# Differential values computed tile by tile in 512-column products, and the last output row tile gathered in SBUF and scaled in two pieces

## The chip, the cores and the metric

One core of one Trainium2 chip runs the whole program. The metric is the device time of one execution in microseconds; the figure given for a kernel is the median of its runs.

## The reference, cut to what matters

Two layers of a hybrid encoder act on a sequence of 512 rows and 1024 columns; a final RMSNorm follows. All values are float32.

```python
for i in range(DEPTH):                                   # 2 layers
    h = rmsnorm(x, norm_mix[i])
    proj = h @ w_in[i]
    qa, ka, va, glu_in, qc, kc, vc, gates = jnp.split(proj, SPLITS, axis=-1)
    ya = diff_attention(qa, ka, va, ...)                 # 4 heads; va is 512 x 512
    yb = conformer_conv(glu_in, ...)
    yc = neighbourhood_attention(qc, kc, vc, rpb[i])     # 8 heads
    ga, gb, gc = jnp.split(jax.nn.sigmoid(gates), 3, axis=-1)
    merged = ga * (ya @ w_br_a[i]) + gb * (yb @ w_br_b[i]) + gc * (yc @ w_br_c[i])
    x = x + merged @ w_o[i]
    h = rmsnorm(x, norm_ffn[i])
    x = x + (silu(h @ w_ffn_gate[i]) * (h @ w_ffn_up[i])) @ w_ffn_down[i]
    h = rmsnorm(x, norm_ple[i])
    x = x + sigmoid(h @ w_ple_gate[i]) * (p[i] @ w_ple_in[i])
return rmsnorm(x, norm_final)
```

The change touches two places of it: `va`, the values of the differential attention, and the very last line, the output rows `x * factor * gain`, where the factor of a row is `(mean(x*x) + EPS) ** -0.5`.

## The kernel before

**Precision.** Every matrix product is made from three: a float32 operand is split into a high half (a rounded copy, made by ACT) and a low half (the difference, made by DVE), and hi x hi, hi x lo and lo x hi are added up in PSUM. `split` is that pair of operations, one on ACT and one on DVE. `weights` loads a block of 128 x 1024 weights by SyncE and splits it; it uses three SBUF pools of three buffers each, `wr` (raw), `wh` and `wl` (the halves), and marks its instructions as 400 steps more urgent than the place where they are written. A buffer is free for the next block when its last reader is done.

**Who sets the order.** TensorE works in the order in which the code is written. The code itself interleaves two kinds of units with the large products: `later` queues an attention unit, and each fourth `chunk` of a product is a `tick` that starts a due unit or takes a running one a step further. A unit of the neighbourhood attention ("natten") is: scores, a softmax on DVE and ACT, transposes, the copies `natten_pt` of the transposed probabilities to SBUF (a high half by ACT, a low half by DVE), the products `natten_av`, and at the end `natten_y`. A unit of the differential attention is built alike. On ACT, DVE and POOL a scheduler orders the instructions by their dependencies and urgency, and each of these engines then works strictly in that order.

**PSUM.** There are eight banks: three named `mm`, two `sc` (scores), two `tr` (transposes), one `av`.

**The values.** `values` (L605) is called by `diff_v` (L830) twice in a layer (L455, L459), each time for two heads, that is 256 columns: four calls in all. A call takes two `mm` banks as accumulators (called `diff_mm`), each for two of the four tiles of 128 rows. The weights come in two loads of four chunks, 1024 columns each. For every chunk and tile there are three products of 256 columns: h's high half with the weights' high half (L621), the same with the weights' low half (L623), h's low half with the weights' high half (L625); 96 in all. When the last is done, four copies on ACT and four subtractions on DVE split the sums into `diff_v`. Around the first call of a layer lie the query and key products of a head (`diff_in`; their rotary embedding makes `diff_rp`, `diff_t` and `diff_kh` on DVE, with `diff_rp` first filled by a DMA), natten units, and behind it the next head's products and a gate (`gatec`).

**The end.** `final` (L1283) makes the last gated embedding and the norm row tile by row tile (t = 0 to 3). `finish` makes a row tile's last 256 columns, adds up its squares, and POOL makes the factor of each row (`ple_rc`, a power). `store` scales the other columns out of PSUM (`low`, columns 0 to 511, and the first half of `pair`, columns 512 to 767) and the last 256 (`v`, times factor and gain), and sends the rows to `out`. For t = 3 that is ACT for columns 0 to 511 with a DMA of its own, and two DVE operations of 256 columns with one SyncE DMA each.

## Time and profile before

| what | before |
|---|---|
| median of 3 runs | 1755.69 us (1755.67 to 1756.33) |
| the profiled execution | 1756.09 us, its span 1754.3 us |
| granted TensorE clock | 0.999 |
| matmuls, weight loads | 8970 each, weight loads 1490.2 us (85%) |
| DVE, ACT, POOL | 1421.7 us (81%), 964.4 us (55%), 104.0 us (6%) |
| DMA | 253.82 MB, 145 GB/s on average |

The span runs from the first to the last instruction of the profiled execution; the execution's own time has 1.8 us around it. Busy shares are averages over the whole span, while a stage is bound by whatever it waits for last; so the stages that the change touches are read on their own below.

### The profile page before, as it was taken

The page shows a single profiled execution, that of the slowest core. Times are in us where ns is not written, and L with a number is a line of the kernel's source. Part 1 is how long each engine was busy: PE and PEld are TensorE (multiplying, and loading weights), DVE is VectorE, ACT ScalarE, POOL GpSimd, SP SyncE. Part 2 cuts the span into 40 slices and gives each one's busy share as a digit, 9 for nine tenths or more (in the row PEclk, how much of TensorE's full clock was granted, in tenths as well). Part 3 has the DMA queues.
Part 4 walks back from the last instruction along what each step waited for, and adds up shares of the span by engine and source line. Part 5 has one row for each costly group of instructions (what it writes and reads, how often), then busy time and mean ns, then how long its engine had stood idle before and what let it go on. Part 6 is the DMA issues. An engine that isn't in the chain of part 4 may idle for free.

```text
span 1754.3 us, 25072 instructions
## 1 busy us (share of the span) xinstructions
PE 1747.3 (100%) x8970; PEld 1490.2 (85%) x8970; DVE 1421.7 (81%) x2346; ACT 964.4 (55%) x1729; POOL 104.0 (6%) x114
## 2 busy tenths in 40 slices
PE   9999999999999999999999999999999999999998
PEld 7888888888888888888888898888888988888887
DVE  7967987998799687797776688889887985977876
ACT  5566545226577275574545665553365763745654
POOL 0000000000121020100000000000001210101000
PEclk9999999999999999999999999999999999999999
DMA  6575641334767365543446655323256764755332
GB/s 230 159 192 158 162 126 46 112 100 140 230 162 186 118 171 155 142 119 131 156 130 164 194 150 153 111 73 96 93 176 199 183 172 121 179 143 157 96 105 97
DMA packets 114781, 253.82 MB, mean 145 GB/s; under 512 B 16864, under 2 KB 23776, under 8 KB 114656
## 3 DMA queue, kind: packets, MB, share of 16 engines
q1 hardware_dynamic: 101264, 227.83, 42.3%
q0 software_dynamic: 12672, 23.07, 8.1%
q8 instruction: 71, 1.16, 0.3%
q10 hardware_dynamic: 720, 1.31, 0.2%
q14 instruction: 54, 0.44, 0.1%
HBM read 215.46 MB, written 7.34 MB: 127 GB/s over the span
## 4 chain that ended last, share of the span: by engine, by line
PE 97%; DVE 1%; DMA 1%; ACT 1%; SPq 0%; issue 0%; POOL 0%; POOLq 0%; ACTq 0%; DVEq 0%
PE ffn_mm L1013 6%; PE ffn_sc L1013 6%; PE ffn_mm L180 4%; PE ffn_mm L179 4%; PE ffn_mm L181 4%; PE ffn_mm L1016 3%; PE ffn_sc L1016 3%; PE mergea_mm L180 2%; PE mergea_mm L181 2%; PE mergea_mm L179 2%; PE ffn_tr L1013 2%; PE natten_mm L179 2%; PE natten_mm L180 2%; PE gateb_mm L180 2%; PE gateb_mm L181 2%; PE gateb_mm L179 2%
## 5 line engine op out<-in xcount | busy, mean ns | idle before, releaser
L160 DVE SCALAR_TENSOR_TENSOR conv_z<-glu_z,pre_par,conv_z 128x512 f32<-128x512 f32 x240 | 179.6, 748 | 3.4
L143 ACT ACTIVATE ffn_wh<-ffn_wr 128x1024 fp32r<-128x1024 f32 (+1 forms) x92 | 92.7, 1021 | 99.5 <-PE ffn_mm L180 63.4
L157 DVE TENSOR_TENSOR ffn_wl<-ffn_wr,ffn_wh 128x1024 fp32r<-128x1024 f32 (+1 forms) x92 | 107.1, 1175 | 20.8 <-ACT ffn_wh L143 20.4
L979 POOL DMA_DIRECT2D ffn_qk<-w_fu x88 | 78.0, 992 | 589.3 <-DMA ffn_qk<-w_fu 323.7
L143 ACT ACTIVATE mergea_wh<-mergea_wr 128x1024 fp32r<-128x1024 f32 (+1 forms) x32 | 27.1, 846 | 96.8 <-PE mergea_mm L180 79.6
L157 DVE TENSOR_TENSOR ffn_t<-ffn_mm,wo_rb 128x512 f32<-128x512 f32 (+1 forms) x46 | 31.1, 677 | 51.6 <-PE ffn_mm L181 51.6
L157 DVE TENSOR_TENSOR ffn_wl<-ffn_qk,ffn_wh 128x1024 fp32r<-128x1024 f32 x44 | 53.7, 1220 | 11.0 <-ACT ffn_wh L143 10.9
L143 ACT ACTIVATE diff_a<-diff_sc,diff_s 128x512 f32<-128x512 f32 x32 | 22.0, 688 | 71.6 <-DVE diff_s L893 71.6
L143 ACT ACTIVATE ffn_wh<-ffn_qk 128x1024 fp32r<-128x1024 f32 x44 | 46.7, 1061 | 26.8 <-PE ffn_mm L180 16.2
L179 PE MATMUL ffn_mm<-ffn_v,ffn_wh 128*128 128x512 f32 x132 | 51.4, 389 | 0.0
L180 PE MATMUL ffn_mm<-ffn_v,ffn_wh 128*128 128x512 f32 x132 | 51.4, 389 | 0.0
L181 PE MATMUL ffn_mm<-ffn_v,ffn_wl 128*128 128x512 f32 x132 | 51.3, 389 | 0.0
L179 PE MATMUL ffn_mm<-ffn_y,ffn_wh 128*128 128x512 f32 x132 | 51.3, 389 | 0.0
L180 PE MATMUL ffn_mm<-ffn_y,ffn_wh 128*128 128x512 f32 x132 | 51.3, 389 | 0.0
L181 PE MATMUL ffn_mm<-ffn_y,ffn_wl 128*128 128x512 f32 x132 | 51.3, 389 | 0.0
L143 ACT ACTIVATE natten_wh<-natten_wr 128x1024 fp32r<-128x1024 f32 x24 | 25.4, 1058 | 42.2 <-issue 15.5
L1013 PE MATMUL ffn_sc<-wo_h,ffn_wh 128*128 128x512 f32 x176 | 48.0, 394 | 0.0
L157 DVE TENSOR_TENSOR ffn_t<-ffn_t,ffn_e 128x256 f32<-128x256 f32 x84 | 46.3, 551 | 1.0 <-ACT ffn_e L143 0.9
L893 DVE TENSOR_REDUCE diff_s<-diff_sc 128x1 f32<-128x512 f32 x64 | 42.1, 683 | 2.2 <-PE diff_sc L800 2.2
L1013 PE MATMUL ffn_mm<-wo_h,ffn_wh 128*128 128x512 f32 x160 | 43.6, 394 | 0.0
L225 POOL TENSOR_TENSOR diff_rc<-diff_sm,pre_power 128x4 f32<-128x4 f32 x8 | 8.9, 1115 | 561.8 <-DVE diff_sm L160 503.2
L143 ACT ACTIVATE natten_b<-natten_b,natten_s 128x256 f32<-128x256 f32 x64 | 30.4, 499 | 20.4 <-DVE natten_s L719 20.3
(894 smaller groups left out, 6050.1 us busy)
## 6 DMA issues: line engine op xcount, KB each, us to landing
ffn_qk<-w_fu POOLq DMA_DIRECT2D x88, 256.0 KB, 6.6
ffn_wr<-w_fg SPq DMA_DIRECT2D x44, 512.0 KB, 4.4
ffn_wr<-w_fd SPq DMA_DIRECT2D x32, 448.0 KB, 3.8
ffn_r<-w_fu SPq DMA_DIRECT2D x44, 256.0 KB, 3.1
ffn_qk<-w_fg SPq DMA_DIRECT2D x44, 256.0 KB, 3.3
ffn_qk<-w_fu SPq DMA_DIRECT2D x44, 256.0 KB, 3.4
natten_wr<-w_in SPq DMA_DIRECT2D x16, 512.0 KB, 4.2
diff_wr<-w_in SPq DMA_DIRECT2D x16, 512.0 KB, 4.3
```

The lines of the kernel that those rows point to most:

```text
L143: i = self.nc.scalar.activation(out, in_, func, **kw)
L157: return self.nc.vector.tensor_tensor(out, a, b, op)
L160: return self.nc.vector.scalar_tensor_tensor(out, a, s, b, op0, op1)
L179: mm(out, wh, ah, start=first, stop=False, **kw)
L180: mm(out, wh, al, start=False, stop=False, **kw)
L181: mm(out, wl, ah, start=False, stop=last, **kw)
L225: nc.gpsimd.tensor_tensor(col, ms, self.power, ALU.pow)
L893: nc.vector.tensor_reduce(out=m[:, u:u + 1], in_=sc, op=ALU.max, axis=AX.X, negate=True)
L979: nc.gpsimd.dma_start(q, wu[:, lo], accum_op=ALU.add)
L1013: mm(out, wh[:, c], bs[k][b], start=first and k == 0, stop=False, skip_group_check=True)
L1016: mm(out[:, 0], wl[:, c], bs[k][b][:, 0], start=False, stop=k == 3, skip_group_check=True)
```

## The change

**The values.** A call now issues both weight loads first. Each raw block of four chunks is split into halves that lie side by side, chunk by chunk: 256 columns of the high half, then 256 of the low one. Two chunks fit into a buffer of `wh` and the other two into one of `wl`, so the two loads fill two buffers of each; a call has four splits of 512 columns each in place of two of 1024. The four row tiles are then made one after the other, each in an `mm` bank of its own (before: two banks in all). A tile has eight products of 512 columns, h's high half with both halves of a chunk, and then eight of 256, h's low half with the weights' high half: 64 products in a call where there were 96. The first 256 columns of the bank then hold hi x hi + lo x hi, the second 256 hi x lo. A tile is taken out as soon as it is done: a copy on ACT and a subtraction on DVE as before, and then one more addition on DVE, which adds the second half of the bank to the low half of `diff_v`.

**The end.** For the last row tile the last 256 columns are multiplied by the gain before the factor is there, and the other 768 are copied from PSUM to SBUF by ACT. With the factor, ACT scales columns 0 to 383 and sends them by its own queue, and DVE scales columns 384 to 1023 in one operation, sent by one SyncE DMA. The scaling of columns 512 to 767 of row tile 2 is written ahead of the last `finish`, and row tile 2's low columns go out by SyncE's queue in place of ACT's.

```diff
--- before.py
+++ after.py
@@ -602,37 +602,39 @@
 
         yield from self.norm(st[0], CB, (3, 1), done)
 
-    def values(self, ap, parts):
+    def values(self, ap):
 
 
         mm = self.nc.tensor.matmul
-        accs = [self.ps("mm", (P, 2, 256)) for _ in range(2)]
-        for o in range(0, KD, 4):
-            wh, wl = self.weights(ap[:, o * 256:(o + 4) * 256], 1024)
-            both = [(k, t) for k in range(o, o + 4) for t in range(4)]
-            if o == 0:
-
-                both.sort(key=lambda kt: kt[1] // 2)
-            for n, (k, t) in enumerate(both):
-                s = slice((k - o) * 256, (k - o + 1) * 256)
-                out = accs[t // 2][:, t % 2, :]
-                ts = slice(t * P, (t + 1) * P)
-
-                mm(out, self.h[k][:, 0, ts], wh[:, s], start=k == 0 and t % 2 == 0,
-                   stop=False, skip_group_check=True)
-                mm(out, self.h[k][:, 0, ts], wl[:, s], start=False, stop=False,
+        ws = []
+        with self.tc.high_priority(offset=min(self.w_ahead, self.tc.cur_priority - self.p0)):
+            for o in range(0, KD, 4):
+                raw = self.sb("wr", [P, 2, 2, 256])
+                self.nc.sync.dma_start(raw.rearrange("p a b c -> p (a b c)"),
+                                       ap[:, o * 256:(o + 4) * 256])
+                for n, tag in enumerate(("wh", "wl")):
+                    w = self.sb(tag, [P, 2, 2, 256], F32R)
+                    self.split(w[:, :, 0], w[:, :, 1], raw[:, n])
+                    ws += [w[:, k] for k in range(2)]
+        vs = []
+        for t in range(4):
+            out = self.ps("mm", (P, 2, 256))
+            hs = [(a[:, 0, t * P:(t + 1) * P], a[:, 1, t * P:(t + 1) * P]) for a in self.h]
+            for k, (hi, lo) in enumerate(hs):
+                mm(out, hi, ws[k], start=k == 0, stop=False, skip_group_check=True)
+                if k % 4 == 3:
+                    self.chunk()
+            for k, (hi, lo) in enumerate(hs):
+                mm(out[:, 0], lo, ws[k][:, 0], start=False, stop=k == KD - 1,
                    skip_group_check=True)
-                mm(out, self.h[k][:, 1, ts], wh[:, s], start=False,
-                   stop=k == KD - 1 and t % 2 == 1, skip_group_check=True)
-                if n % 2:
+                if k % 4 == 3:
                     self.chunk()
-        vs = []
-        for acc in accs:
-            v = self.sb("v", [P, 2, 512], F32R)
-            for t in range(2):
-                for hi, lo, a in parts(v[:, t], acc[:, t]):
-                    self.split(hi, lo, a)
-            vs.append(v)
+            if t % 2 == 0:
+                v = self.sb("v", [P, 2, 512], F32R)
+                vs.append(v)
+            hi, lo = v[:, t % 2, 0:256], v[:, t % 2, 256:512]
+            self.split(hi, lo, out[:, 0])
+            self.tt(lo, lo.bitcast(F32), out[:, 1], ALU.add)
         return vs
 
     def natten_in(self, pr, st, ys):
@@ -829,7 +831,7 @@
 
     def diff_v(self, g, st):
         self.phase = "diff"
-        st["v", g] = self.values(self.a["w_va"][self.i, g], lambda v, a: ((v[:, 0:256], v[:, 256:512], a),))
+        st["v", g] = self.values(self.a["w_va"][self.i, g])
 
     def diff_unit(self, head, qt, st4, k2, st, box, ys):
 
@@ -1332,22 +1334,34 @@
             summed.append(self.stt(ms, s, 1.0 / D, part[:, t:t + 1], ALU.mult, ALU.add))
             col = self.sb("rc", [P, 1])
             nc.gpsimd.tensor_tensor(col, ms, self.power[:, 0:1], ALU.pow)
+            if t == 3:
+                self.behind(self.tt(rows[t][:, 768:], v, self.gain, ALU.mult), summed[t])
             vs.append(v)
             columns.append(col)
 
+        def lower(t):
+            nc.vector.tensor_scalar(rows[t][:, 512:768], pair[t][:, 0:256], columns[t], None,
+                                    ALU.mult)
+
         def store(t):
-            col, two = columns[t], pair[t]
+            col = columns[t]
             r, out = rows[t], self.a["out"][t * P:(t + 1) * P]
+            if t == 3:
+                c, d = slice(0, 384), slice(384, D)
+                self.act(r[:, 0:512], low[t], AF.Copy)
+                self.act(r[:, c], r[:, c], AF.Copy, scale=col)
+                nc.scalar.dma_start(out[:, c], r[:, c])
+                nc.vector.tensor_scalar(r[:, d], r[:, d], col, None, ALU.mult)
+                nc.sync.dma_start(out[:, d], r[:, d])
+                return
             self.act(r[:, 0:512], low[t], AF.Copy, scale=col)
-            nc.scalar.dma_start(out[:, 0:512], r[:, 0:512])
+            (nc.sync if t == 2 else nc.scalar).dma_start(out[:, 0:512], r[:, 0:512])
             i = self.stt(r[:, 768:], vs[t], col, self.gain, ALU.mult, ALU.mult)
             if t == 2:
                 self.behind(i, summed[3])
-            if t == 3:
-                nc.sync.dma_start(out[:, 768:], r[:, 768:])
-            nc.vector.tensor_scalar(r[:, 512:768], two[:, 0:256], col, None, ALU.mult)
-            c = slice(512, 768 if t == 3 else D)
-            nc.sync.dma_start(out[:, c], r[:, c])
+            if t < 2:
+                lower(t)
+            nc.sync.dma_start(out[:, 512:], r[:, 512:])
 
         pair, low, pgs, vs, columns, summed = [], [], [], [], [], []
         places = ("av", "mm", "av", "sc")
@@ -1388,6 +1402,9 @@
             pgs.append(pg)
             if t == 1:
                 finish(0)
+            if t == 3:
+                lower(2)
+                self.act(rows[t][:, 512:768], pair[t][:, 0:256], AF.Copy)
             if t:
                 finish(t)
             if t in (1, 2):
```

The order of instructions moves with it. The first place is DVE in the first call of `values` in layer 0. `diff_rp` and `diff_t` are the rotary embedding of the key product just made, `diff_wl_307` is the low half of the weights of the next key product (head 1), `conv_z` belongs to the convolution, and `natten_y` to the natten unit in between. Before:

```order
L160 SCALAR_TENSOR_TENSOR conv_z_81_370<-glu_z_68_321,pre_par_1_67,conv_z_81_370 128x512
L157 TENSOR_TENSOR diff_rp_265_1482<-diff_rp_265_1482,diff_r_235_1323 128x512
L157 TENSOR_TENSOR diff_t_266_1488<-diff_t_266_1488,diff_rp_265_1482 128x512
L157 TENSOR_TENSOR diff_wl_307_1766<-diff_wr_305_1764,diff_wh_306_1765 128x1024
L157 TENSOR_TENSOR diff_rp_264_1481<-diff_t_266_1488,diff_kh_267_1493 128x512
L157 TENSOR_TENSOR natten_y_194_1079<-natten_mm_274_1561,natten_y_194_1079 64x512
```

After; `diff_mm_275` and `diff_mm_277` are the banks of the first and the second row tile, and `diff_v_276` is what is taken out of them:

```order
L160 SCALAR_TENSOR_TENSOR conv_z_81_370<-glu_z_68_321,pre_par_1_67,conv_z_81_370 128x512
L157 TENSOR_TENSOR diff_v_276_1538<-diff_mm_275_1521,diff_v_276_1538 128x256
L157 TENSOR_TENSOR diff_rp_265_1482<-diff_rp_265_1482,diff_r_235_1323 128x512
L157 TENSOR_TENSOR diff_v_276_1538<-diff_v_276_1538,diff_mm_275_1521 128x256
L157 TENSOR_TENSOR diff_t_266_1488<-diff_t_266_1488,diff_rp_265_1482 128x512
L157 TENSOR_TENSOR diff_v_276_1538<-diff_mm_277_1542,diff_v_276_1538 128x256
L157 TENSOR_TENSOR diff_v_276_1538<-diff_v_276_1538,diff_mm_277_1542 128x256
L157 TENSOR_TENSOR diff_rp_264_1481<-diff_t_266_1488,diff_kh_267_1493 128x512
L157 TENSOR_TENSOR natten_y_194_1079<-natten_mm_278_1559,natten_y_194_1079 64x512
```

The subtraction and the added addition of the first two tiles now stand between the steps of the rotary embedding; the addition of the first tile comes behind `diff_rp_265`. The subtraction for the next key weights is gone from here.

The second place is ACT at the end of the same call. `natten_b`, `natten_e` and `natten_pt` are the softmax and the probabilities of the natten units, `gatec_wh` the weights of the gate, `diff_wh_338` those of the product after it. Before:

```order
L143 ACTIVATE diff_v_288_1685<-diff_mm_269_1505 128x256
L143 ACTIVATE gatec_wh_325_1864<-gatec_wr_324_1863 128x1024
L143 ACTIVATE diff_v_288_1685<-diff_mm_269_1505 128x256
L143 ACTIVATE natten_b_283_1656,natten_s_285_1660<-natten_b_283_1656,natten_s_285_1660 128x256 x2
L143 ACTIVATE diff_v_289_1690<-diff_mm_270_1506 128x256
L143 ACTIVATE natten_b_283_1656<-natten_b_283_1656,natten_s_285_1660 128x256 x2
L143 ACTIVATE natten_e_284_1657,natten_s_285_1660<-natten_e_284_1657,natten_s_285_1660 128x256 x2
L143 ACTIVATE diff_v_289_1690<-diff_mm_270_1506 128x256
L143 ACTIVATE natten_pt_297_1721<-natten_tr_296_1716 128x512
L143 ACTIVATE natten_e_284_1657<-natten_e_284_1657,natten_s_285_1660 128x256 x2
L143 ACTIVATE natten_pt_299_1729<-natten_tr_298_1724 128x512
L143 ACTIVATE diff_wh_338_1929<-diff_wr_337_1928 128x1024
```

After; `diff_mm_284` and `diff_mm_286` are the third and the fourth tile, `diff_wh_308` the key weights of head 1 (that is `diff_wh_306` of before, which stood ahead of these rows), `diff_wh_340` is `diff_wh_338` of before, `natten_pt_299` and `natten_pt_301` are 297 and 299 of before:

```order
L143 ACTIVATE diff_v_285_1620<-diff_mm_284_1603 128x256
L143 ACTIVATE diff_wh_308_1743<-diff_wr_307_1742 128x1024
L143 ACTIVATE gatec_wh_327_1842<-gatec_wr_326_1841 128x1024
L143 ACTIVATE natten_e_280_1572<-natten_e_280_1572,natten_s_281_1575 128x256 x2
L143 ACTIVATE diff_v_285_1620<-diff_mm_286_1624 128x256
L143 ACTIVATE natten_b_287_1641,natten_s_289_1645<-natten_b_287_1641,natten_s_289_1645 128x256 x2
L143 ACTIVATE natten_e_288_1642,natten_s_289_1645<-natten_e_288_1642,natten_s_289_1645 128x256 x2
L143 ACTIVATE natten_b_287_1641<-natten_b_287_1641,natten_s_289_1645 128x256 x2
L143 ACTIVATE natten_e_288_1642<-natten_e_288_1642,natten_s_289_1645 128x256 x2
L143 ACTIVATE natten_pt_299_1699<-natten_tr_298_1694 128x512
L143 ACTIVATE diff_wh_340_1907<-diff_wr_339_1906 128x1024
L143 ACTIVATE natten_pt_301_1707<-natten_tr_300_1702 128x512
```

The split of the key weights has moved behind the copy of the third tile and stands next to that of the gate's weights, ahead of the next natten softmax; and the weights of the product after the gate come between the two copies of `natten_pt`, where they came behind both.

The third place is DVE a little later, at the same two `natten_pt`. Before:

```order
L157 TENSOR_TENSOR diff_v_289_1690<-diff_mm_270_1506,diff_v_289_1690 128x256
L157 TENSOR_TENSOR natten_pt_297_1721<-natten_tr_296_1716,natten_pt_297_1721 128x512
L157 TENSOR_TENSOR natten_pt_299_1729<-natten_tr_298_1724,natten_pt_299_1729 128x512
L157 TENSOR_TENSOR diff_wl_339_1930<-diff_wr_337_1928,diff_wh_338_1929 128x1024
L157 TENSOR_TENSOR diff_t_302_1751<-diff_rp_300_1744,diff_r_234_1321 128x512
```

After:

```order
L157 TENSOR_TENSOR diff_v_285_1620<-diff_v_285_1620,diff_mm_286_1624 128x256
L727 RECIPROCAL natten_s_289_1645<-natten_s_289_1645 128x2
L157 TENSOR_TENSOR natten_pt_299_1699<-natten_tr_298_1694,natten_pt_299_1699 128x512
L157 TENSOR_TENSOR diff_wl_341_1908<-diff_wr_339_1906,diff_wh_340_1907 128x1024
L157 TENSOR_TENSOR natten_pt_301_1707<-natten_tr_300_1702,natten_pt_301_1707 128x512
L157 TENSOR_TENSOR diff_t_304_1729<-diff_rp_302_1722,diff_r_234_1321 128x512
```

The low half of these weights, `diff_wl`, now comes between the two low halves of `natten_pt`.

## The prediction

> **What bounds the kernel now.** I read the page's head, its chain that ended last, and then the busy time by stretch, at the first call of `values` in each layer and at the end.
>
> ```profile
> span 1754.3 us, 25072 instructions
> PE 1747.3 (100%) x8970; PEld 1490.2 (85%) x8970; DVE 1421.7 (81%) x2346; ACT 964.4 (55%) x1729; POOL 104.0 (6%) x114
> PE 97%; DVE 1%; DMA 1%; ACT 1%; SPq 0%; issue 0%; POOL 0%; POOLq 0%; ACTq 0%; DVEq 0%
> ...
> 141.70:165.30 23.60, 23.60 (x168) 22.10 (x166) 18.25 (x43) 15.55 (x39) 0.00 (x0) 1.00 0.58 162
> 1011.10:1034.70 23.60, 23.60 (x168) 22.11 (x167) 18.76 (x44) 16.24 (x40) 0.00 (x0) 1.00 0.59 163
> ```
>
> TensorE works the whole span; 97% of the chain is its own. The two lower rows (length, then busy time of PE, weight loads, DVE, ACT, POOL, granted clock, DMA) cover the first call and what follows it: PE 23.60 of 23.60 us, clock 1.00. So time is won only by less work on PE, and each wait that PE newly meets is lost for good, since no slack behind it takes it up. DVE (18.25) and ACT (15.55) are off the path, but PE is fed through them.
>
> **Step 1, the products.** Per call 96 products of 256 columns become 32 of 512 and 32 of 256. Columns are the same (24,576); what falls is a cost per product. Durations in the groups overlap, so I use distances between starts.
>
> ```profile
> 141.90 0.28 PE L623 MATMUL diff_mm<-diff_wl,glu_h 128*128 128x256 f32 x1
> ...
> 147.42 0.28 PE L625 MATMUL diff_mm<-diff_wh,glu_h 128*128 128x256 f32 x1
> 702.42 0.39 PE L180 MATMUL ffn_mm<-ffn_v,ffn_wh 128*128 128x512 f32 x1
> ...
> 705.59 0.39 PE L179 MATMUL ffn_mm<-ffn_y,ffn_wh 128*128 128x512 f32 x1
> 1641.18 0.93 PE ffn_mm L1013 x4
> 1642.11 0.48 PE ffn_mm L1016 x4
> ```
>
> From 141.90 to 147.42 lie 46 steps: 0.120 us each. From 702.42 to 705.59 lie 14: 0.2264. A call now costs 96 x 0.120 = 11.52 us. After: 32 x 0.2264 + 32 x 0.120 = 11.08 us, 0.44 less. The last two rows are the same mixture in the FFN, four wide and four narrow in 0.93 + 0.48 = 1.41 us; eight such are 11.28, 0.24 less. Bounds 0.24 and 0.44; I take the middle, 0.35 to 0.37, and with four calls **-1.5 us** (-1.0 to -1.8).
>
> The row says that a merged pair saves 2 x 120 - 226 = 14 ns. The Trainium skill, "TensorE: Matmul & The Clock Gate", section "Back-to-back issue gap", gives a warm gap of N/2.4 + 2.5 ns, by which a pair would save 2.5 ns, and 128 pairs 0.3 us instead of 1.5; the trace disagrees with it (120 ns for 256 columns where the formula has 109), and the trace decides.
>
> **Step 2, the bank of the first tile (wait A).** Four tiles now take four "mm" banks where two did, and there are three; the natten unit between takes one too. The third tile therefore needs the first one's bank, which is free only after the added DVE addition. That addition stands behind the rope product `diff_rp`, as the order shows.
>
> ```profile
> 147.54 1.07 PE L745 MATMUL natten_mm<-natten_pt,natten_v 128*128 128x192 f32 x8
> ...
> 149.42 0.28 PE L621 MATMUL diff_mm<-diff_wh,glu_h 128*128 128x256 f32 x1
> 148.71 0.69 DVE L157 TENSOR_TENSOR diff_rp<-diff_rp,diff_r 128x512 f32<-128x512 f32 x1 [0.73 <-DMA diff_rp<-diff_rp]
> 161.17 0.75 DVE L157 TENSOR_TENSOR diff_v<-diff_mm,diff_v 128x256 fp32r<-128x256 f32 x2
> 1017.41 0.69 DVE L157 TENSOR_TENSOR diff_rp<-diff_rp,diff_r 128x512 f32<-128x512 f32 x1
> 1011.11 0.36 PE L621 MATMUL diff_mm<-diff_wh,ple_h 128*128 128x256 f32 x1
> ```
>
> Layer 0: the product starts at 148.71, when its DMA lands; the next DVE operation can follow 0.60 us on, at 149.31, takes 0.42 (two take 0.75, so 0.33 apart) and ends at 149.73; PE restarts at about 149.8. PE arrives earlier: 141.70 + two tiles of 2.79 + the natten rows (147.54 to 149.42, 1.88) + 0.08 at the first product = 149.2. **Wait 0.6 us.** Layer 1: no DMA wait there, but a new DVE subtraction stands ahead, so 1017.41 + 0.33 + 0.60 + 0.42 = 1018.76, PE at 1018.85; it arrives at 1011.11 + 5.58 + 1.88 + 0.08 = 1018.65. **Wait 0.2.** Bounds 0 and, if the landing slips by half a microsecond, 1.2 and 0.7. In the second call of each layer only score banks stand between; t3 asks for t0's bank two tiles later, some 5.6 us of cover. I cost it at nothing.
>
> **Step 3, the queue that feeds the next natten unit (wait B).** Both weight halves are now held to the last tile. So the split of the weights after next (k of head 1), which ran at 147.74 while ACT had nothing else, moves behind the third tile's copy, next to that of gate c, and both stand in ACT's and DVE's queue ahead of the natten softmax.
>
> ```profile
> 147.74 1.06 ACT L143 ACTIVATE diff_wh<-diff_wr 128x1024 fp32r<-128x1024 f32 x1 [1.67 <-PE diff_mm L625]
> 156.05 0.49 ACT L143 ACTIVATE natten_e<-natten_e,natten_s 128x256 f32<-128x256 f32 x1
> 162.68 0.58 ACT L143 ACTIVATE natten_pt<-natten_tr 128x512 fp32r<-128x512 f32 x1
> 163.15 0.90 ACT L143 ACTIVATE natten_e<-natten_e,natten_s 128x256 f32<-128x256 f32 x2
> 163.95 0.58 ACT L143 ACTIVATE natten_pt<-natten_tr 128x512 fp32r<-128x512 f32 x1
> 164.57 0.69 DVE L157 TENSOR_TENSOR natten_pt<-natten_tr,natten_pt 128x512 fp32r<-128x512 f32 x1 [0.59 <-ACT natten_pt L143]
> 165.52 1.23 DVE L157 TENSOR_TENSOR diff_wl<-diff_wr,diff_wh 128x1024 fp32r<-128x1024 f32 x1 [0.26 <-ACT diff_wh L143]
> 166.66 0.69 DVE L157 TENSOR_TENSOR diff_t<-diff_rp,diff_r 128x512 f32<-128x512 f32 x1
> 165.22 0.96 PE L745 MATMUL natten_av<-natten_pt,natten_v 128*128 128x192 f32 x7
> 1033.26 0.69 DVE L157 TENSOR_TENSOR natten_pt<-natten_tr,natten_pt 128x512 fp32r<-128x512 f32 x1 [0.59 <-ACT natten_pt L143]
> 1034.63 0.36 PE L745 MATMUL natten_av<-natten_pt,natten_v 128*128 128x192 f32 x2
> ```
>
> Before, the second `natten_pt` is done at 165.26, and PE's `natten_av`, which reads it from its fifth product on, starts at 165.22: a cover of some 0.4 us. After: up to the exponentials DVE trades one weight subtraction (1.14 from start to start) for four short operations (1.3), so the last of them still ends at about 156.5 on ACT. Then by ACT's new order: tile copy 0.28 and k's split, which ends at 156.5 + 0.28 + 1.06 = 157.84; DVE makes its low half and that of gate c, 2 x 1.14, and reaches the next unit's scores at 160.1; the first exponential starts at 160.5; four of 0.49 and four scalings of 0.40 make 164.06; first `natten_pt` copy 0.48; then the weights of the next product (now ahead of the second copy) to 165.60; on DVE their low half, also ahead of it now, 165.64 + 1.14 = 166.78; second `natten_pt` 0.69, ready at 167.47. PE: 165.22 + 0.6 - 0.37 = 165.45 at its first product, 165.95 at the sixth. **Wait 1.5 us.** In layer 1 DVE stood 0.7 us earlier against PE (1033.26 to 1034.63, against 164.57 to 165.22), but loses 0.33 to the new subtraction, and PE loses only 0.2 at A: 1.5 again. Bounds per layer: 0 where the chain holds, 2.2 if PE waits from the first `natten_pt` on.
>
> **Step 4, the end.** The last row tile keeps its factor on time (the two additions on DVE lie under POOL's power). Then two DVE operations become one of 640 columns, and ACT scales 384 instead of 512.
>
> ```profile
> 1749.86 0.48 DVE L160 SCALAR_TENSOR_TENSOR ple_y<-ple_a,ple_rc,ple_b 128x256 f32<-128x256 f32 x1 [0.43 <-POOL ple_rc L1334]
> 1750.26 0.48 DVE L1348 TENSOR_SCALAR ple_y<-ple_tr,ple_rc 128x256 f32<-128x256 f32 x1
> 1750.79 0.41 SPq L1350 DMA_DIRECT2D out<-ple_y  x1
> ...
> L551 DVE TENSOR_SCALAR conv_z<-glu_z,pre_par 128x512 f32<-128x512 f32 x8 | 4.3, 542 | 0.0
> out<-ple_y SPq DMA_DIRECT2D x3, 256.0 KB, 2.4
> out<-ple_y SPq DMA_DIRECT2D x2, 128.0 KB, 2.1
> ```
>
> Scaled from the same operation in SBUF (542 ns for 512 columns), 640 take 0.68 us; at the rate of the 256 columns out of PSUM, 1.20. From 1749.86 the last DMA is issued at 1750.58 to 1751.10 instead of 1750.79: -0.2 to +0.3; nearest row, -0.2. It carries 320 KB instead of 128, and the rows put 0.3 us on 128 KB more, at most 0.45 here, though all the bytes together are the same. **0.0 us**, from -0.3 to +0.7.
>
> **Sum.** -1.5 + (0.6 + 0.2) + (1.5 + 1.5) + 0.0 = +2.3 us. The profiled execution, 1754.3 of span in 1756.09, would become 1758.4; the median of the runs shown, 0.4 lower, 1755.69, becomes **1758.0**. That is 0.13%; 0.2% (3.5 us) is about what a measurement of this kernel can tell from no change.
>
> **Rivals.**
> *The cover holds.* If ACT and DVE get through the new order about 2 us sooner than the rows add up to, neither wait arises and the products' gain stays: 1755.7 - 1.5 = 1754.2. For it: DVE has 5 us idle in that stretch (18.25 of 23.60), ACT 8. Against it: the chain is one of dependent operations, and 0.4 us was all the cover there was. 15%, cases in which only one of the two layers waits among them.
> *The rope's DMA lands late, slower.* A is decided by the landing at 148.71. SP's order shifts by a DMA around both places; each 0.5 us later adds 0.5 at A in each layer, while B moves along with it. From 0.6 us on the whole is 0.2% slower: 1.0 us gives 2.3 + 2.0 = +4.3, 1760.0. For it: DVE waited there already (0.73); against it: the issues that count stand before the call and hardly move. 17%.
> *The change does not shorten the products.* If a wide product costs what two narrow ones do (0.240), only the waits are left: +3.8, less 0.4 as A shrinks when PE comes later: 1759.1. Nothing in the rows supports it; it gets 4%. The gap in the skill's page, with 0.3 us gained, would give nearly this, +3.3.
> *More than the sum allows at the end, or a gain elsewhere:* 2%.
>
> **Numbers.** The forecast has 62%: waits between 2.6 and 4.5 us, so 1756.8 to 1759.0 for its own part. The range reaches down to a part of the covered case and up to most of the late landing: 1754.8 to 1759.9. Slower by over 0.2% (above 1759.2): the late landing and a part of the third rival, 0.20; faster by over 0.2% (below 1752.2): 0.02; within: 0.78.
>
> **What would show it.** Step 1: distances of 0.226 to 0.235 us in the wide products of `diff_mm`, and 11.1 to 11.3 us of PE per call. A: PE idle 0.2 to 0.8 us at the third tile of the first call of each layer, ended by DVE's `diff_v`; none in the second calls. B: PE idle over 1 us within `natten_av` near 166 and 1036, ended by DVE's `natten_pt`, with `diff_wl` just ahead of it on DVE. Step 4: the last DMA's issue about 1.0 us after POOL's power ends. I am wrong if PE runs through 141 to 168 without a gap, or if a wait shows in the second calls.

## The result, and the profile after

| | before | changed |
|---|---|---|
| median of 19 runs | 1756.21 us (1755.39 to 1756.74) | 1759.33 us (1758.75 to 1759.81) |
| span of the profiled execution | 1754.3 us | 1757.1 us |
| ratio of the two | | 1.0018, 95% interval 1.0012 to 1.0024 |

The changed kernel is 3.1 us slower (the interval allows 2.1 to 4.2). That is under 0.2%, but the interval does not reach 1.0000, so it is a loss and not noise. The forecast was 2.3 us more. Of the 3.1 us, 0.3 lie outside the span: the execution's own time has 2.1 us around it in every run of the changed kernel, and 1.8 before. e7, e12, e14 and e15 below have 2.1 as well, the other experiments 1.8 to 1.9; what makes the difference the runs do not show.

The head of the page of the changed kernel, and then the complete list of what TensorE waited for (us in total, times, longest):

```profile
span 1757.1 us, 24856 instructions
PE 1747.5 (99%) x8842; PEld 1484.5 (84%) x8842; DVE 1427.2 (81%) x2370; ACT 966.4 (55%) x1739; POOL 104.0 (6%) x114
...
PE natten_av L747 <- DVE natten_pt L157: 2.0, 2, 1.0
PE pre_av L331 <- DVE pre_zeror L404: 1.1, 1, 1.1
PE diff_mm L624 <- DVE diff_v L157: 0.2, 1, 0.2
```

128 matmuls are gone, yet PE's busy time has not fallen (1747.3 before): a busy PE is not a PE at its peak, because the ends of matmuls are modelled. So all lengths below are distances between starts. What the list does show is where new waits are: `natten_av`, once in each layer, ended by DVE's `natten_pt`, and a small one at `diff_mm`, ended by DVE's `diff_v`. (`pre_av` stands in the list of before too.) None is in the second calls of `values`.

**The first call of `values`, from its first product to the scores behind it,** in the timeline of PE; the rows are those at which the kind of work changes. Before, layer 0 and layer 1:

```profile
141.69 0.36 PE L621 MATMUL diff_mm<-diff_wh,glu_h 128*128 128x256 f32 x1
155.18 0.28 PE L800 MATMUL natten_sc<-natten_qk 128*128 128x256 f32 x1
1024.59 0.28 PE L800 MATMUL natten_sc<-natten_qk 128*128 128x256 f32 x1
```

In the changed kernel:

```profile
142.16 0.71 PE L624 MATMUL diff_mm<-diff_wh,glu_h 128*128 128x512 f32 x2
149.59 0.28 PE L802 MATMUL natten_sc<-natten_x,natten_qk 128*128 128x256 f32 x1
149.86 0.70 PE L624 MATMUL diff_mm<-diff_wh,glu_h 128*128 128x512 f32 x2
155.52 0.28 PE L802 MATMUL natten_sc<-natten_qk 128*128 128x256 f32 x1
1012.10 0.71 PE L624 MATMUL diff_mm<-diff_wh,ple_h 128*128 128x512 f32 x2
1020.00 0.70 PE L624 MATMUL diff_mm<-diff_wh,ple_h 128*128 128x512 f32 x2 [0.20 <-DVE diff_v L157]
1025.64 0.28 PE L802 MATMUL natten_sc<-natten_qk 128*128 128x256 f32 x1
```

Layer 0: 13.49 us before, 13.36 after. Layer 1: 13.48 before (from 1011.11), 13.54 after. The last score product before the third tile starts at 149.59 and the tile at 149.86, 0.15 later than the 0.12 that a product of 256 columns takes; the list above has no entry for that, so a wait of this size has to be read from the starts.

**The natten unit behind the call.** ACT, DVE and PE of the changed kernel, layer 0; the timeline rows as they follow on each engine:

```profile
164.20 0.58 ACT L143 ACTIVATE natten_pt<-natten_tr 128x512 fp32r<-128x512 f32 x1
164.67 1.05 ACT L143 ACTIVATE diff_wh<-diff_wr 128x1024 fp32r<-128x1024 f32 x1
165.62 0.58 ACT L143 ACTIVATE natten_pt<-natten_tr 128x512 fp32r<-128x512 f32 x1
164.80 0.69 DVE L157 TENSOR_TENSOR natten_pt<-natten_tr,natten_pt 128x512 fp32r<-128x512 f32 x1 [1.91 <-ACT natten_pt L143]
165.75 1.23 DVE L157 TENSOR_TENSOR diff_wl<-diff_wr,diff_wh 128x1024 fp32r<-128x1024 f32 x1 [0.26 <-ACT diff_wh L143]
166.90 0.68 DVE L157 TENSOR_TENSOR natten_pt<-natten_tr,natten_pt 128x512 fp32r<-128x512 f32 x1
165.57 1.07 PE L747 MATMUL natten_av<-natten_pt,natten_v 128*128 128x192 f32 x5
167.63 0.59 PE L747 MATMUL natten_av<-natten_pt,natten_v 128*128 128x256 f32 x3 [1.00 <-DVE natten_pt L157]
168.07 0.49 PE L737 MATMUL natten_tr<-pre_ident,natten_b 128*128 128x128 f32 x3
```

`natten_av` from its first product to the transposes takes 2.50 us (165.57 to 168.07); before, it took 0.92 (165.22 to 166.14). In layer 1 it is the same: 1035.69 to 1038.19 against 1034.63 to 1035.55. PE stands in front of its sixth product until DVE has made the second low half, and DVE makes the weights' low half first. This is 1.58 us a layer.

**The end.** PE's last products, DVE's last addition, the last power on POOL and SyncE's last issue; of the rows of before, the last one, the issue at 1750.79, stands in the prediction:

```profile
1750.30 0.60 PE L1319 MATMUL ple_sc<-pre_ident,ple_h 128*128 128x128 f32 x4
1750.48 0.42 DVE L157 TENSOR_TENSOR ple_a<-ple_t,ple_tr 128x256 f32<-128x256 f32 x1 [0.36 <-ACT ple_y L143]
1751.71 0.59 POOL L1336 TENSOR_TENSOR ple_rc<-ple_sm,pre_power 128x1 f32<-128x1 f32 x1 [2.43 <-DVE ple_sm L160]
1752.92 0.33 SPq L1355 DMA_DIRECT2D out<-ple_y  x1
```

and before:

```profile
1748.02 0.60 PE L1317 MATMUL ple_sc<-pre_ident,ple_h 128*128 128x128 f32 x4
1749.17 0.65 POOL L1334 TENSOR_TENSOR ple_rc<-ple_sm,pre_power 128x1 f32<-128x1 f32 x1 [2.19 <-DVE ple_sm L160]
```

From PE's last products to the power: 1.15 us before, 1.41 after. From the power to the last SyncE issue: 1.62 and 1.21. From that issue to the end of the span: 3.5 and 4.2. Together 6.3 and 6.8, so the end costs 0.5 us. In the changed kernel ACT issues a last transfer of its own 0.06 us behind SyncE's, and it lands later than SyncE's (see e10).

Two things in these single profiles are chance. PE starts its first layer's work 0.46 us later in the profile of the changed kernel (0.2 to 1.0 us later in the experiments' profiles too, though none of them changes the beginning). And the profile of before holds a wait of its own at 175.19, which the changed kernel and the experiments lack:

```profile
175.19 0.50 PE L800 MATMUL diff_sc<-diff_qk 128*128 128x512 f32 x1 [0.23 <-ACT diff_e L143]
```

With the products around it that is 0.6 us. The two nearly cancel in the spans, and the steps below are compared without them.

### The profile page after: what moved, and what is told of

Read it like the earlier page. It is cut to its first block, busy times and chain, and to the rows that moved or that the text cites. A ratio compares the mean times of both kernels' runs of the same rounds, so it can differ in the third digit from the quotient of the medians.

```text
span 1757.1 us, 24856 instructions
## 1 busy us (share of the span) xinstructions
PE 1747.5 (99%) x8842; PEld 1484.5 (84%) x8842; DVE 1427.2 (81%) x2370; ACT 966.4 (55%) x1739; POOL 104.0 (6%) x114
## 3 DMA queue, kind: packets, MB, share of 16 engines
q8 instruction: 70, 1.15, 0.3%
## 4 chain that ended last, share of the span: by engine, by line
PE 95%; DVE 2%; ACT 2%; issue 0%; DMA 0%; SPq 0%; POOLq 0%; DVEq 0%; ACTq 0%
PE ffn_mm L1015 6%; PE ffn_sc L1015 6%; PE ffn_mm L181 4%; PE ffn_mm L179 4%; PE ffn_mm L180 4%; PE ffn_mm L1018 3%; PE ffn_sc L1018 3%; PE mergea_mm L180 2%; PE mergea_mm L181 2%; PE mergea_mm L179 2%; PE ffn_tr L1015 2%; PE diff_sc L802 2%; PE gatec_mm L180 2%; PE gatec_mm L179 2%; PE gatec_mm L181 2%; PE gateb_mm L180 2%
```

## The experiments

All ratios are to the kernel before, run on the same chip beside them; its medians were 1755.99, 1756.08 and 1756.23 us in the three series.

| kernel | median us | ratio (95%) |
|---|---|---|
| e1_values_only | 1758.81 | 1.0016 (1.0007 to 1.0025) |
| e2_end_only | 1756.69 | 1.0003 (0.9995 to 1.0012) |
| e4_evict_first | 1758.53 | 1.0015 (1.0006 to 1.0024) |
| e7_query_later | 1756.26 | 1.0001 (0.9992 to 1.0010) |
| e9_all_three | 1759.34 | 1.0021 (1.0012 to 1.0030) |
| e13_query_first | 1757.84 | 1.0009 (1.0000 to 1.0018) |
| e12_pairs | 1765.27 | 1.0051 (1.0039 to 1.0064) |
| e10_end_two | 1756.38 | 1.0000 (0.9991 to 1.0009) |
| e14_three_fixes | 1756.19 | 0.9999 (0.9990 to 1.0008) |
| e15_narrow | 1757.40 | 1.0008 (0.9999 to 1.0017) |

Differences of half a microsecond lie within these intervals; where one decides, it is read from the trace.

**e1_values_only and e2_end_only: which half costs?** Each takes one half of the change and the other half of the kernel before: e1 has `finish`, `store` and the end of `final` as before, e2 has `values` as before and the new end, of which the core is

```diff
+                self.act(r[:, 0:512], low[t], AF.Copy)
+                self.act(r[:, c], r[:, c], AF.Copy, scale=col)
+                nc.scalar.dma_start(out[:, c], r[:, c])
+                nc.vector.tensor_scalar(r[:, d], r[:, d], col, None, ALU.mult)
+                nc.sync.dma_start(out[:, d], r[:, d])
...
```

> The new values with the old end. Theory (products give 0.35 us a call, the third tile's bank takes back 0.2 to 0.4 a layer, the second natten_pt 1.5 a layer, and in layer 0 some 0.6 of it is won back where PE waited before at diff_sc): +1.8 us against the kernel before, ratio 1.0010, and in the trace the gaps at the third tile and in natten_av as in the changed kernel. Rival 'it is the end' (longer last transfer, ACT's extra copies): about -1 us, ratio 0.9995, since then the values alone gain.

> The old values with the new end. Theory: +0.5 us, ratio 1.0003 (the last transfer lands 0.6 us later after its issue, the additions before the last factor 0.2 later, the issue itself 0.4 earlier). Rival 'it is the end': +2 to +3 us, ratio 1.0015. A third reading, that the new end gains as its two pieces suggest: -0.3 us.

Measured: 2.8 us for the values alone and 0.7 for the end alone, against their own before. The values carry the loss, and the rival "it is the end" falls. The expected 1.8 for the values was 1.0 too low. 0.6 of that I had counted as won back at `diff_sc`: e2, with the old values, lacks that wait as well, so it belongs to the one profile of before and not to the change. The other 0.4 is within the interval. In e1's list of PE's waits stand the same three entries as above. In e2 PE's last products to the end of the span take 6.8 us (1748.50 to 1755.3) as in the changed kernel, in e1 6.4 (1750.18 to 1756.6).

**e7_query_later: one pair swapped.** Two operations change places in a layer, `natten_pt` and the weight split ahead of it, once on ACT and once on DVE.

```diff
             self.low = self.split(hi[:, :n], lo[:, :n], raw[:, :n], then)
+            if self.hold:
+                for x, y in zip(self.both, self.copied[-3]):
+                    self.behind(x, y)
+                self.hold = False
...
+        self.hold = True
         self.diff_in(2, sd, ya)
```

> The changed kernel with one pair swapped on ACT and one on DVE in each layer: the split of the weights behind the gate (diff_wh, diff_wl) stands behind the second natten_pt, as in the kernel before, and not ahead of it. Theory (the queue ahead of natten_pt makes the wait, and this split alone is 1.1 us of it): natten_av runs through, 1.3 to 1.5 us less in a layer, of which layer 0 gives back up to 0.6 at diff_sc: +0.2 to +0.9 us against before, ratio 1.0001 to 1.0005. Rival 'the weights held to the last tile make it' (the key weights' split next to the gate's, 1.1 us, ahead of the softmax): the wait only shrinks to some 0.8 us, ratio about 1.0013. Rival 'natten_av waits for something else, the engine named is done long before': ratio 1.0018.

The timelines of DVE and PE at the same place:

```profile
164.94 1.29 DVE L158 TENSOR_TENSOR natten_pt<-natten_tr,natten_pt 128x512 fp32r<-128x512 f32 x2 [1.92 <-ACT natten_pt L144]
166.38 1.23 DVE L158 TENSOR_TENSOR diff_wl<-diff_wr,diff_wh 128x1024 fp32r<-128x1024 f32 x1
165.72 1.16 PE L756 MATMUL natten_av<-natten_pt,natten_v 128*128 128x192 f32 x8
166.71 0.49 PE L745 MATMUL natten_tr<-pre_ident,natten_b 128*128 128x128 f32 x3
```

`natten_av` takes 0.99 us (0.92 before, 2.50 in the changed kernel), and the time is 0.3 us above before, where the changed kernel stood 3.1 above. In the order of ACT and of DVE nothing else moved, and the key weights' split still stands ahead of the softmax. So the position of one split, with the buffers held as they were, decides the whole of this wait. The softmax being late is what leaves no room for that split; by itself it costs less than 0.1 us here.

**e12_pairs: why did the order change at all?** Here no order is set by hand. The tiles go in pairs, and the first load's buffers come free earlier.

```diff
+        for p in range(2):
+            outs = [self.ps("mm", (P, 2, 256)) for _ in range(2)]
+            for o in (0, 4):
+                for out, t in zip(outs, (2 * p, 2 * p + 1)):
...
+                    for k, hi, lo in hs:
+                        mm(out, hi, ws[k], start=k == 0, stop=False, skip_group_check=True)
...
```

> The changed kernel with its four tiles made in pairs: for two tiles the first load's chunks, then the second load's, so that the first load's buffers come free a tile earlier (after the third and fourth tile's first halves and not after all). No order is set by hand. Theory (the buffers held to the last tile delay the key weights' split, that delays the softmax, and so the next query's split gets ahead of the second natten_pt): the natten_av wait vanishes or shrinks below 0.3 us in each layer; the third tile's bank comes free later and may cost up to 0.5 us more in each layer: 0 to +1.5 us against before, ratio 1.0000 to 1.0009. Rival 'the holding has nothing to do with it': the wait in natten_av stays at 1.4 us, ratio 1.0018 or more.

The timeline rows of ACT (the key weights, then the second `natten_pt` and the next query's weights) and of PE, and PE's longest wait from the list:

```profile
154.66 1.04 ACT L143 ACTIVATE diff_wh<-diff_wr 128x1024 fp32r<-128x1024 f32 x1
163.85 0.58 ACT L143 ACTIVATE natten_pt<-natten_tr 128x512 fp32r<-128x512 f32 x1
164.33 1.05 ACT L143 ACTIVATE diff_wh<-diff_wr 128x1024 fp32r<-128x1024 f32 x1
165.63 1.08 PE L748 MATMUL natten_av<-natten_pt,natten_v 128*128 128x192 f32 x8
...
PE diff_mm L627 <- DVE diff_v L157: 5.6, 2, 3.0
```

With the key weights split at 154.66 instead of 156.79, the scheduler puts the next query's split behind the second `natten_pt` of its own accord, and `natten_av` runs through in 8 products without a gap. That fits the chain that the theory claims: buffers held, split late, softmax late, order turned. But e12 also changes when the tiles end and are taken out, so that the holding by itself turns the order is likely and not shown alone. The time, however, is 9.2 us worse, far outside what was expected: in the second calls both tiles of a pair end together, the next pair needs their banks at once, and the additions stand in DVE's queue behind the rotary embedding and the probabilities of the next units. That wait I had put at 0.5 us; it is 2.6 and 3.0 in the two layers. Behind each of the two waits the granted clock is halved for 3.41 us (the last section has a row of it), which costs some 1.7 us more each time.

**e4_evict_first: the bank of the first tile.**

```diff
+            with self.tc.high_priority(offset=min(self.w_ahead, self.tc.cur_priority - self.p0)):
-            self.split(hi, lo, out[:, 0])
-            self.tt(lo, lo.bitcast(F32), out[:, 1], ALU.add)
+                self.split(hi, lo, out[:, 0])
+                self.tt(lo, lo.bitcast(F32), out[:, 1], ALU.add)
```

> The changed kernel with the taking-out of each tile (copy, subtraction, addition) marked 400 steps more urgent, so that on DVE the addition stands ahead of the rope product. Theory: PE no longer waits at the third tile of the first call of a layer, 0.66 us less in both layers together, if the wait in natten_av stays as it is: +2.4 us against before, ratio 1.0014. Rival 'the bank is short whatever DVE does' (the natten unit between the tiles takes the bank): the gap at the third tile stays, ratio 1.0018.

The timeline of PE in layer 0:

```profile
141.98 0.71 PE L624 MATMUL diff_mm<-diff_wh,glu_h 128*128 128x512 f32 x2
149.53 0.63 PE L624 MATMUL diff_mm<-diff_wh,glu_h 128*128 128x512 f32 x2
155.12 0.28 PE L803 MATMUL natten_sc<-natten_qk 128*128 128x256 f32 x1
```

The stretch takes 13.14 us instead of 13.36, and the first product of the third tile is no longer slow (0.63 for its pair, 0.70 with the wait). So the wait is the place of the taking-out in DVE's queue, not a lack of banks. The time (2.5 us above before, the changed kernel 3.1) can't carry this: 0.3 of the 0.6 us lie outside the span, and e4 moves the taking-out of every tile. Its list shows the wait in `natten_av` in another form, 1.1 us ended by ACT's `natten_pt` and 0.7 by DVE's. e14 below, which moves the first tile alone, is the narrower test, and its third tile has no wait either.

**e9_all_three and e13_query_first: all at once.** Tiles first, old end, and the splits of gate and query (e9) or of the query alone (e13) behind the second `natten_pt`.

> New values with the tiles taken out first, the gate's and the next query's weight splits behind the second natten_pt, and the old end. Theory (three separate charges, each taken away): neither wait, the old end, so only the products' 0.35 us a call stay: -1.4 us against before, ratio 0.9992. Rival 'a new wait takes their place' (the gate's weights or the rotary embedding of the next head late): ratio 1.0000 to 1.0010, with a gap in the trace between 166 and 185 us.

> As the kernel before it in this call, but the gate's split stays ahead of the softmax; only the next query's split is held behind the second natten_pt. Theory: the first wait gone, the second reduced from 1.4 us to what ACT's two splits ahead of the softmax still cost, 0 to 0.5 us in a layer: -1.4 to -0.4 us against before, ratio 0.9992 to 0.9998. If it equals the kernel before it, the swap alone is the whole of the second wait.

e9 missed: the time is 3.3 us above before. Its list of PE's waits has neither of the two old entries, but two new ones, and the timeline shows the worse of them:

```profile
PE diff_sc L813 <- ACT diff_e L144: 1.9, 2, 1.0
PE diff_sc L813 <- ACT diff_a L144: 1.1, 2, 0.6
...
183.76 0.50 PE L813 MATMUL diff_sc<-diff_qk 128*128 128x512 f32 x1 [0.97 <-ACT diff_e L144]
184.34 0.63 PE L186 MATMUL diff_mm<-glu_h,diff_wh 128*128 128x512 f32 x1
184.76 0.63 PE L187 MATMUL diff_mm<-glu_h,diff_wh 128*128 128x512 f32 x1
```

By their starts the scores of the differential unit behind the natten unit now come some 2 us later in each layer. On ACT the two splits of the values' weights (181.91 and 182.43) stand between that unit's two exponentials, `diff_a` at 181.23 and `diff_e` at 182.95; in the changed kernel they stand behind both (`diff_e` 181.05, splits 181.73 and 182.25). How the two moved splits bring this about was not tried. The rival "a new wait takes their place" is right here. The profiled execution of e9 (1761.11) is one of the longer ones, which the last section explains in part. e13, which moves one split less, missed its forecast of 0.4 to 1.4 us below before: it stands 1.8 us above. Its list has 0.4 us at `natten_av` in both layers together, and 0.5 at `diff_sc`; the rest is spread over delays too small for the list.

**e10_end_two: the last transfer.**

```diff
-                nc.vector.tensor_scalar(r[:, d], r[:, d], col, None, ALU.mult)
-                nc.sync.dma_start(out[:, d], r[:, d])
+                for d in (slice(384, 704), slice(704, D)):
+                    nc.vector.tensor_scalar(r[:, d], r[:, d], col, None, ALU.mult)
+                    nc.sync.dma_start(out[:, d], r[:, d])
```

> The old values with the new end, but DVE's 640 columns in two operations of 320 with one 160 KB transfer each instead of 320 KB. Read in the trace from the last power on POOL to the end of the span: before 5.1 us, new end 5.4. Theory 'the size of the last transfer sets it' (320 KB land 4.2 us after their issue, 128 KB 3.5): 5.0 to 5.2. Rival 'all of the last row's 512 KB leave at once and share the engines': 5.4 or more. The time: +0.3 to +0.7 us against before, too small to tell by the clock alone.

The power on POOL starts at 1749.11 and the span ends at 1754.1: 4.99 us, where the new end has 5.39 in e2 and 5.4 in the changed kernel. That is what the theory gave, but the size of SyncE's transfer is not the whole of it. In the changed kernel the last issue is ACT's, and ACT's transfer lands last. This is its timeline row, and then two rows of the DMA list of the changed kernel, whose last number is the time from issue to landing in us:

```profile
1752.98 0.35 ACTq L1353 DMA_DIRECT2D out<-ple_y  x1
out<-ple_y SPq DMA_DIRECT2D x1, 320.0 KB, 2.5
out<-ple_y ACTq DMA_DIRECT2D x1, 192.0 KB, 2.9
```

Before, the last issue was one of SyncE's 128 KB, which took 2.1 us (the row is in the prediction). ACT's 192 KB take 2.7 us in e2 and 3.0 in e7, both beside SyncE's 320 KB, but 2.3 in e10 and 2.2 in e14, where SyncE sends two pieces of 160 KB. So ACT's transfer is slow beside the one large transfer; whether they share something, as the rival has it, the runs do not show. In e14, which splits SyncE's transfer in the same way, the power to the end takes 5.36; its first transfer is issued 0.71 us after DVE's start on it (0.41 in e10), and what delayed that issue the trace does not say. The first part of the loss is clear, though: the 1.41 us from PE's last products to the power are the same in the four kernels with ACT's copy ahead of the last additions (1.40 in e10), and 1.14 in e14, where the copy is behind them.

**e14_three_fixes and e15_narrow: the products by themselves.** e14 is the changed kernel with e7's swap, the first tile alone taken out early, and the mended end. e15 is the same with two narrow products for each wide one.

```diff
-                mm(out, hi, ws[k], start=k == 0, stop=False, skip_group_check=True)
+                mm(out[:, 0], hi, ws[k][:, 0], start=k == 0, stop=False, skip_group_check=True)
+                mm(out[:, 1], hi, ws[k][:, 1], start=False, stop=k == KD - 1,
+                   skip_group_check=True)
```

> The changed kernel with each charge taken away with as little moved as possible: the next query's split behind the second natten_pt; only the first tile of a layer's first call taken out ahead of the rope product on DVE; at the end DVE's scaling in two operations of 320 with a transfer each, and ACT's copy of columns 512 to 767 behind the last addition. Theory: the products' 0.35 us a call stay, at the end 6.1 us from TensorE's last products to the end of the span (before 6.3, changed 6.8): -1.4 us against before, ratio 0.9992, no wait on PE in natten_av or at the third tile. Rival 'a new wait takes their place': ratio 1.0000 or more, with a gap in the trace.

> The same kernel, but each product of 512 columns as two of 256, so that a call has 96 products again, with the same weights' layout and tiles. Theory (a wide product saves 11 to 14 ns against two narrow ones): 0.35 us more in a call, +1.4 us against the kernel before it in this call. Rival 'the wide products save only the 2.5 ns each that the Trainium skill's gap gives': +0.3 us. The scheduler moves a few operations on ACT and DVE with it; if a wait arises there, the calls' lengths in the trace decide.

PE's timeline of e14, and then of e15, from the first product of the call to the scores behind it:

```profile
142.23 0.71 PE L632 MATMUL diff_mm<-diff_wh,glu_h 128*128 128x512 f32 x2
155.36 0.28 PE L812 MATMUL natten_sc<-natten_qk 128*128 128x256 f32 x1
```

```profile
141.95 0.36 PE L632 MATMUL diff_mm<-diff_wh,glu_h 128*128 128x256 f32 x1
155.43 0.28 PE L814 MATMUL natten_sc<-natten_qk 128*128 128x256 f32 x1
```

13.13 us with wide products, 13.48 with narrow ones: 0.35 us a call, or 11 ns for each of its 32 wide products. The times agree: e15 is 1.2 us above e14, where four calls make 1.4, though e15's list also has a wait of 0.3 us at `natten_tr` that e14 lacks. The Trainium skill, "TensorE: Matmul & The Clock Gate", section "Back-to-back issue gap", gives N/2.4 + 2.5 ns for the gap of an isolated matmul; an estimate from that page is 2.5 ns saved for each merged pair, 0.3 us in all. These runs do not agree with it.

e14 lies level with the kernel before (0.9999), not 1.4 us below. 0.3 of the 1.4 lie outside the span. The end takes 6.5 us (1747.30 to 1753.8) and not the 6.1 expected. And PE, which has no wait on the list except the one at the start, is late by 0.1 to 0.2 us in several places (`natten_av` takes 1.07 us in layer 1, from 1034.08 to 1035.15, where 0.92 would do). No version beats both kernels beyond doubt.

## Why the prediction came out as it did

The forecast was right in sign and in the mechanism of its largest term, and 0.8 us too low (1759.33 against 1758.0; the other 0.5 is the median of before, 1756.21 in the longer series in place of 1755.69). By its steps, all from starts in the traces:

| step | predicted us | measured us |
|---|---|---|
| 1, products, four calls | -1.5 | -1.4 (0.36 and 0.34 in the two first calls, before against e14: 13.49 to 13.13, 13.48 to 13.14) |
| 2, third tile, layer 0 and 1 | +0.6, +0.2 | +0.23, +0.40 (13.36 and 13.54 against e14's 13.13 and 13.14) |
| 3, natten_av, layer 0 and 1 | +1.5, +1.5 | +1.58, +1.58 |
| 4, the end | 0.0 | +0.5 |
| sum | +2.3 | +2.9; the runs: +3.1, of which 0.3 outside the span |

*Step 1* holds. The middle of its two bounds, 0.24 and 0.44, is 0.34 us a call and 1.4 in all, not the 1.5 that it took, and the middle is what was measured.

*Step 2* named the right wait in the right calls, and e4 and e14 show that the place of the taking-out behind the rope product makes it. Its sizes were off, one up and one down, so that 0.8 against 0.63 in all is partly luck. In layer 0 it rested on the landing of the rope's DMA, taken from one row of before. In the changed kernel that DMA did not hold DVE at all, in these rows of DVE's timeline:

```profile
148.70 0.68 DVE L157 TENSOR_TENSOR diff_rp<-diff_rp,diff_r 128x512 f32<-128x512 f32 x1
149.30 0.41 DVE L157 TENSOR_TENSOR diff_v<-diff_v,diff_mm 128x256 fp32r<-128x256 f32 x1
```

The rope product starts at 148.70 without an idle time before it, although everything else in this profile is 0.46 us later than before. The landing is not fixed: in e2, e10 and e15 DVE waits for it by 0.30, 0.59 and 0.30 us. In layer 1 PE arrived where it was expected, and restarted 0.16 us later than the sum had it, with a slow first product on top.

*Step 3* carried the forecast, and its size came out within 0.1 us in each layer. That step 2 was 0.4 off in layer 0 did not spoil it, since the earlier rope product moved PE and the chain on DVE and ACT alike: ACT copies the third tile at 156.51, where the working had 156.5, in a profile that runs 0.46 us late. The working gave three charges ahead of the second `natten_pt`: the key weights' split, the gate's split beside it, and the next query's split between the two copies. e7 shows that the last is enough to make or break the wait; e12, where the first comes 2.1 us earlier and the order of before returns, fits that the first turns the order, but it changes more than that. Step 3 told both as one chain. Of the rivals, "the cover holds" falls with the list of waits, and "the rope's DMA lands late" with the two rows above.

*Step 4* is the step that failed, within its bounds (-0.3 to +0.7) but away from the value taken, 0.0 against 0.5. The issue did come earlier, by 0.4 us and not 0.2, because DVE's 640 columns took 0.55 us and not 0.68. But "the two additions on DVE lie under POOL's power" overlooked ACT's new copy of columns 512 to 767: the last addition waits 0.36 us for it, and the factor comes 0.26 us later. And the landing came later: from SyncE's last issue to the end of the span 0.7 us more, where at most 0.45 was allowed for and then dropped with the words that the bytes together are the same. The step priced SyncE's 320 KB alone; what lands last is ACT's 192 KB, for which it has no term.

## What to carry to other kernels

A change that shortens work on the bounding engine must also be priced by what it does to the queues of the engines that feed it: here 1.4 us of gain on TensorE met 3.2 us of waits that came from one weight split changing places with a copy on ACT and DVE. Holding a buffer for longer cost little by itself here (e7); what costs is the order that the scheduler makes, so compare the instruction order around every point where a buffer comes free. And after moving a long operation out of one unit's queue, look into the next unit's: e9 won both waits back and lost more there. At the end of a kernel, price every queue's last transfer, since the one that lands last need not be the largest.

## What the runs showed of the hardware that was not expected

A gap on TensorE can be followed by a stretch at half the clock. In e9, after the gap of 0.97 us, eight products of 512 columns went 0.43 us apart where 0.227 is usual (184.34 to 184.76 in the rows above shows the first). The granted clock, the third number from the end in these rows of busy time by stretch, was 0.50 for 3.41 us. The first row is e9's, the second e12's, behind its wait in layer 0:

```profile
184.31:187.72 3.41, 3.41 (x9) 2.67 (x8) 3.15 (x6) 1.59 (x5) 0.00 (x0) 0.50 0.51 154
205.71:209.12 3.41, 3.41 (x12) 2.83 (x11) 2.13 (x4) 1.75 (x3) 0.00 (x0) 0.50 0.69 159
```

A third such stretch, of the same length and clock, stands in e12 at 1079.52, behind the wait in layer 1. In e9 eight times 0.2 is 1.6 us. e9's eleven runs fall into two groups: six from 1758.6 to 1759.3 us with a mean granted clock of 1.000, and five from 1760.6 to 1761.4 with 0.999. The profiled one is among the five, so the stretch is likely what parts the groups; the other runs have no profile to show it. Even the shorter ones are 2.5 us or more above before.

In the changed kernel the gap in `natten_av`, as long as e9's, was not followed by it (clock 1.00 behind it), nor was the same pair of gaps in layer 1 of e9; what decides was not tried.
